# Reading TensorE's moving operands in turn from two halves, in a two-part fp32 transformer on one core

## The chip, the cores and the metric

One Trainium2 chip, of which the program uses one core. The metric is the device time of one execution in microseconds (us). Before the change it is 1760.87 us, the median of three runs (1760.87 to 1761.02).

## What is computed

256 tokens of width 1024 pass through two layers of a first block and two of a second, all in fp32:

```python
def first_block(...):          # twice
    h = rmsnorm(x, g_pre_mix[l])
    z = h @ w_in[l]            # 2660 columns: three attentions' q, k, v, the gates, the low-rank parts
    mix = concatenate([moba, fox, mla, dilated], axis=-1)
    x = x + rmsnorm(mix @ w_out[l], g_post_mix[l])
    h = rmsnorm(x, g_pre_ffn[l])
    f = silu(h @ w_gate[l]) * (h @ w_up[l])          # 2816 columns each
    x = x + rmsnorm(f @ w_down[l], g_post_ffn[l])

def second_block(...):         # twice
    x = x + 0.5 * rms_norm(swiglu(rms_norm(x, ...), ffn1), ...)
    x = x + rms_norm(hybrid_mixer(rms_norm(x, ...), w_in[l], ...), ...)   # gated convolution and pooling
    x = x + 0.5 * rms_norm(swiglu(rms_norm(x, ...), ffn2), ...)
```

Six gated feed-forward networks of width 2816 hold most of the multiplications.

## The kernel before, in words

Every weight matrix is cut, on the host, into units of 128 x 1024 fp32 words (`_layout`), which the kernel reads in the order of their use. A unit goes by DMA into one of five `raw` tiles. ScalarE copies it to fp32r as the high part (`splitter`), and VectorE subtracts that from the raw words to get the low part (`lows`). The high parts lie in tiles `wh` (and `xh` inside a feed-forward network), the low ones in `wl` and `xl`. The activations are split in the same way: `hX` holds the normalized tokens, for each of eight blocks of 128 features 256 words of high part and then 256 of low part; `fH`/`fL`, `tH`/`tL`, `mH`/`mL` and `dH`/`dL` hold later activations.

A product of fp32 accuracy is three fp32r products that accumulate in one PSUM bank. There are three forms of them:

- `mm3` has the tokens as the stationary operand and a stretch of weights (512, 256, 356 or 384 columns) as the moving one: high by high, high by low, low by high. The bank then holds tokens by output columns.
- `pair` has 128 columns of weights as the stationary operand and the tokens as the moving one: 512 columns of `hX` (high and low part) against the high weights, and 256 columns (high part) against the low weights. The bank then holds output columns by tokens, in two halves of 256, which `gather` (and `part` in the feed-forward network) add: ScalarE copies the second half to SBUF, VectorE adds the first half to it.
- `mm3f` does the same as three products of 256 columns, for the pooling groups of the second block.

Each MATMUL has a LDWEIGHTS of its own, which loads its 128 stationary columns.

A feed-forward network takes its 2816 columns in 11 chunks of 256. Chunk 0 is made with `mm3` (`tokens`), chunks 1 to 10 with `pair` (`features`: four banks of eight pairs each), and the products with the down weights (`down`, `mm3`) for chunk c-2 stand behind the features of chunk c. A planner, class `Order`, runs the whole program through a model of the engines when it is built, and writes down each engine's order; it takes the cost of a matmul from its number of columns and of an ACT or DVE instruction from its number of elements. Tiles are taken from lists, the longest idle first.

Where the high part of a unit lies in its `wh` tile depends on what the unit is for. The tile has 16 words (`LEAD`) more than a unit. Units that are stationary operands, counted in `add_units(n, True)`, begin at the tile's start; units that are moving operands begin 16 words, 64 bytes, later. The small tiles `sm` and the tiles `gap` are allocated between the weight tiles so that stationary units of `wh` begin 64 bytes past a multiple of 128 bytes and all others at a multiple:

```python
H = w[0][:, :1024] if i in ahead else w[0][:, LEAD:]
```

Of the kernel before, what the change touches and what calls it, by code (L numbers as in the profile page):

```python
# [11 lines left out]
F32 = mybir.dt.float32  # L12
# [22 lines left out]
ROW_G = 10  # L35
ROW_BG = 12
NSLOT = 9
LEAD = 16
NRAW = 5
NMORE = 5  # L40
TABLE = {AF.Exp: 0, AF.Ln: 1, AF.Silu: 2, AF.Sin: 2, AF.Sigmoid: 3}
# [57 lines left out]
def _meet(a, b):  # L99
# [12 lines left out]
            if not (i0 < j1 and j0 < i1):  # L112
                return False
    return True


class Unit(tuple):
    pass


class Order:
# [160 lines left out]
def body(ctx, tc, x, positions, wu, wm, wq_up, wkv_up, rows, feat, gfeat, cst, cid, out, nsub=99):  # L282
# [41 lines left out]
    def add(o, a, b):  # L324
        return tt(o, a, b, OP.add)
# [52 lines left out]

    hpair = one.tile([P, 16 * S], F32R, name="hX").rearrange("p (k t) -> p k t", k=8)
    hat = [hpair[:, :, :S], hpair[:, :, S:]]  # L380


    smt, wmain = [], []
    for i in range(NSLOT):
        smt += [one.tile([P, 4], F32, name=f"sm{i}_{j}") for j in range(6)]
        wmain.append((one.tile([P, LEAD + 1024], F32R, name=f"wh{i}"), one.tile([P, 1024], F32R, name=f"wl{i}")))
    rawt = [one.tile([P, 1024], F32, name=f"raw{i}") for i in range(NRAW)]
    scrt = [one.tile([P, 512], F32, name=f"scr{i}") for i in range(6)]
    xt = [one.tile([P, D], F32, name=f"x{h}") for h in range(2)]
# [8 lines left out]
    mhalf = one.tile([P, 1], F32, name="mhalf")  # L398
    banks = Slots(ck, [psp.tile([P, 512], F32, name=f"bank{i}") for i in range(8)])
    scr = Slots(ck, scrt)  # L400
    smt += [smp.tile([P, 4], F32, name=f"sm_{i}") for i in range(10)]
    smn = [0]

    def small(n=1):
# [3 lines left out]
    def row_ap(i, n):  # L408
        return bass.AP(tensor=rows.tensor, offset=rows.offset + i * D, ap=[[0, P], [1, n]])

    def mm3(o, lh, ll, wh, wl, start, stop):
        yield mm(o, lh, wh, start, False)
        yield mm(o, lh, wl, False, False)
        yield mm(o, ll, wh, False, stop)

    def mm3f(o, wh, wl, xh, xl, start, stop):
        yield mm(o, wh, xh, start, False)
        yield mm(o, wh, xl, False, False)
        yield mm(o, wl, xh, False, stop)

    def pair(o, wh, wl, x, start, stop):

        yield mm(o, wh, x, start, False)
        yield mm(o[:, :S], wl, x[:, :S], False, stop)

    def gather(bs_, dst=None):
        s = None
        if dst is None:
            s = yield scr
            dst = [s[:, :S], s[:, S:]]  # L430
        for b, d in zip(bs_, dst):
            yield act(d, b[:, S:], AF.Copy)
            yield add(d, d, b[:, :S])
            banks.put(b)
        return s


    more = {"slots": [], "end": 0}
    freed = [Task()]
    plan, ahead = [], set()  # L440
    st = {"dma": 0, "split": 0, "use": 0}
    split_out = {}

# [12 lines left out]
            return B_SPLIT[0] if ahead <= 0 else B_SPLIT[1] if ahead < 2 else B_SPLIT[3] if ck.urgent else B_SPLIT[2]  # L456
        return f

    def lows(i, u):
        H, L = u  # L460
        for _, pp, a, b in plan[i]:
            yield sub(L[:pp, a:b], rawt[i % NRAW][:pp, a:b], H[:pp, a:b], split_bias(i))
        split_out[i] = u
        ck.set(ck.flag("unit", i))
        st["split"] += 1
        issue()
# [14 lines left out]

    def splitter():
        for i in range(len(plan)):
            w = yield from slot(i)
            H = w[0][:, :1024] if i in ahead else w[0][:, LEAD:]
            yield ck.flag("raw", i)
            for _, pp, a, b in plan[i]:
                yield act(H[:pp, a:b], rawt[i % NRAW][:pp, a:b], AF.Copy, split_bias(i))
            if i:
                yield ck.flag("unit", i - 1)  # L490
            u = Unit((H, w[1]))
            u.slot = w
            ck.spawn(lows(i, u))

    def unit():
        i = st["use"]
# [15 lines left out]
    def done(*us):  # L512
        for u in us:
            for w in (u.got if isinstance(u, Units) else [u]):
                (more["slots"] if w.slot[0].name.startswith("xh") else wmain).append(w.slot)
        wake()


# [137 lines left out]
    def ffn(n_, half, nxt, fp):  # L656
# [3 lines left out]
        ck.spawn(gain(n_))  # L660
        ft_ = Slots(ck, [(fp.tile([P, 2, S], F32R, name=f"fH{i}"), fp.tile([P, 2, S], F32R, name=f"fL{i}"))
                         for i in range(3)])
        more["slots"] = [(fp.tile([P, 64 - LEAD], F32, name=f"gap{i}"), fp.tile([P, LEAD + 1024], F32R, name=f"xh{i}"),
                          fp.tile([P, 1024], F32R, name=f"xl{i}"))[1:] for i in range(NMORE)]
        R = fp.tile([P, S], F32, name="R")
        more["end"] = st["use"] + 6 * NCH
        wake()
# [37 lines left out]
        def part(c, i):  # L705

            for m in range(2):
                yield ck.flag("part", n_, c, i, m)
                if m == 0:
                    s = yield scr  # L710
                b = hold.pop((c, i, m))
                d = s[:, m * S:(m + 1) * S]
                yield act(d, b[:, S:], AF.Copy)
                yield add(d, d, b[:, :S])
                banks.put(b)
            hold[c, i] = s

        def fchain(c, g, u):
# [432 lines left out]
    def block2(n_, l, ap, nxt):  # L1151
# [137 lines left out]
        def group(g, tp):  # L1289
            yield tp  # L1290
            b = yield banks
            dH, dL = dT[g]
            H, L = wg.got[g // 2]
            for m in range(2):
                o = b[:, m * S:(m + 1) * S]
                for k in range(2):
                    w = slice((g % 2) * 512 + k * 256 + m * P, (g % 2) * 512 + k * 256 + (m + 1) * P)
                    yield from mm3f(o, H[:, w], L[:, w], dH[:, k, :], dL[:, k, :], k == 0, k == 1)
            ds_.put((dH, dL))
            if g == 3:  # L1300
                done(wg)
            z = yield scr
            for m in range(2):
                j = 2 * g + m
                yield act(z[:, m * S:(m + 1) * S], b[:, m * S:(m + 1) * S], AF.Identity,
                          scale=ft[:, 24 + j:25 + j], bias=bs[:, j:j + 1])
            banks.put(b)
            yield from evac_split(two(z), zX[0][:, 2 * g:2 * g + 2, :], zX[1][:, 2 * g:2 * g + 2, :])
            scr.put(z)
# [80 lines left out]
    subs = subs[:nsub]  # L1390
    nu = 0

    def add_units(n, pairs=False):
        nonlocal nu
        for _ in range(n):
            if pairs:
                ahead.add(len(plan))
            plan.append([(wu[nu // 2][:, (nu % 2) * 1024:(nu % 2 + 1) * 1024], P, 0, 1024)])
            nu += 1

    for kind, l, _ in subs:
        if kind == "f":
            add_units(4)
            for c in range(1, NCH):
                add_units(4, True)
                add_units(2 if c > 1 else 0)
            add_units(4)
        elif kind == "b2":
            add_units(16)
            add_units(34, True)  # L1410
            add_units(24)
        else:
            for i in range(4):
                if l or i:
                    plan.append([(wm[l, i], P, 0, 712)])
                else:
                    plan.append([(wm[l, i][:, a:a + 356], P, a, a + 356) for a in (0, 356)])
            add_units(4 + 4 + 4)
            plan.append([(wq_up[l, :P], P, 0, 384), (wq_up[l, P:], 64, 384, 768)])
            plan.append([(wkv_up[l], P, 0, 512)])  # L1420
            add_units(4 + 2 + 8)
# [55 lines left out]
    return w.reshape(k // P, P, n).transpose(1, 0, 2)  # L1477


def _layout(i):  # L1480
    f = {k: np.ascontiguousarray(v) for k, v in i.items()}
    units = []

    def full(w, n):
        t = _kt(w)
        for c in range(w.shape[1] // n):
            kk = 1024 // n
            for a in range(t.shape[1] // kk):
                units.append(t[:, a * kk:(a + 1) * kk, c * n:(c + 1) * n].reshape(P, 1024))

    def ffn(g, u, d):
        tg, tu, td = _kt(g), _kt(u), _kt(d)

        def gu(c):
            if c:
                for t in (tg, tu):
                    units.extend(t[:, :, c * 256 + j * P:c * 256 + (j + 1) * P].reshape(P, 1024) for j in range(2))
                return
            t = np.concatenate([tg[:, :, c * 256:(c + 1) * 256], tu[:, :, c * 256:(c + 1) * 256]], axis=2)
            units.extend(t[:, 2 * a:2 * a + 2].reshape(P, 1024) for a in range(4))  # L1500

        def dn(c):
            units.extend(td[:, 2 * c + a].reshape(P, 1024) for a in range(2))
        gu(0)
        gu(1)
        for c in range(2, NCH):
# [5 lines left out]
    for l in range(DEPTH):  # L1512
# [6 lines left out]
        t = _kt(f["w_out"][l])  # L1519
        for k in range(0, 8, 2):  # L1520
            for n in range(2):
                units.append(t[:, k:k + 2, n * 512:(n + 1) * 512].reshape(P, 1024))
        ffn(f["w_gate"][l], f["w_up"][l], f["w_down"][l])
    for l in range(DEPTH):
        gu = f["ffn1_w_gate_up_2"][l]
# [2 lines left out]
        full(w[:, 4096:], 512)  # L1528
        for j in range(4):
            for o in (1024, 2048, 0):  # L1530
                full(w[:, o + j * 256:o + (j + 1) * 256], 256)
        t = f["w_pool_group_2"][l].reshape(4, 2, P, 256).transpose(2, 0, 1, 3).reshape(P, 2048)
        units += [t[:, :1024], t[:, 1024:]]
        full(w[:, 3072:4096], 256)
        full(f["w_conv_out_2"][l], 512)
        full(f["w_pool_out_2"][l], 512)
        full(f["w_o_2"][l], 512)
# [2 lines left out]
    wu = np.empty((len(units) // 2, P, 2048), np.float32)  # L1540
    for n, u in enumerate(units):
        wu[n // 2, :, (n % 2) * 1024:(n % 2 + 1) * 1024] = u
    wm = np.stack([_kt(np.ascontiguousarray(f["w_in"][l][:, 1536:1892])).reshape(P, 4, 712).transpose(1, 0, 2)
                   for l in range(DEPTH)])
    rows = np.zeros((ROW_BG + 4, D), np.float32)
    names = [(n, l) for l in range(DEPTH) for n in ("mix", "ffn")]
# [13 lines left out]
    for l in range(DEPTH):  # L1560
        for k in range(3):
# [2 lines left out]
        feat[l, :, 32:40] = f["b_pool_group_2"][l].reshape(8, P).T  # L1564
    cst, cid = _constants()
    return dict(x=f["x"], positions=f["positions"], wu=wu, wm=np.ascontiguousarray(wm),
                wq_up=f["w_mla_q_up"], wkv_up=f["w_mla_kv_up"], rows=rows, feat=feat, gfeat=gfeat, cst=cst, cid=cid)


def _constants():  # L1570
# [35 lines left out]
```

## Time and profile before

| what | value |
|---|---|
| median of three runs | 1760.87 us |
| the profiled execution's own time | 1760.87 us |
| its span, first to last instruction | 1759.1 us |
| granted TensorE clock over the span | 1.000 |
| PE busy | 1749.5 us, 99% |
| DVE busy | 1265.9 us, 72% |
| ACT busy | 1031.8 us, 59% |
| DMA | 187 GB/s in the mean |

PE is the matmuls of TensorE and PEld its weight loads. Busy time is the union of the instructions' spans; matmuls overlap in the profile because each is shown to the end of its pipeline, so the mean duration of a matmul is longer than its place in the stream. How long one matmul holds TensorE is read from the distance between the starts of matmuls that follow each other. In a matmul's names (bank<-hX,wh) the moving operand stands first and the stationary one second.

### The profile page before, as it was taken

The page shows a single profiled execution, that of the slowest core. Times are in us where ns is not written, and L with a number is a line of the kernel's source. Part 1 is how long each engine was busy: PE and PEld are TensorE (multiplying, and loading weights), DVE is VectorE, ACT ScalarE, POOL GpSimd, SP SyncE. Part 2 cuts the span into 40 slices and gives each one's busy share as a digit, 9 for nine tenths or more (in the row PEclk, how much of TensorE's full clock was granted, in tenths as well). Part 3 has the DMA queues.
Part 4 walks back from the last instruction along what each step waited for, and adds up shares of the span by engine and source line. Part 5 has one row for each costly group of instructions (what it writes and reads, how often), then busy time and mean ns, then how long its engine had stood idle before and what let it go on. Part 6 is the DMA issues. An engine that isn't in the chain of part 4 may idle for free.

```text
span 1759.1 us, 25148 instructions
## 1 busy us (share of the span) xinstructions
PE 1749.5 (99%) x9417; PEld 1494.9 (85%) x9417; DVE 1265.9 (72%) x1927; ACT 1031.8 (59%) x1749; POOL 36.9 (2%) x72
## 2 busy tenths in 40 slices
PE   9999999999999999999999999999999999999998
PEld 7788888888888888888888888888888888888887
DVE  6878665877866586656888686668665688868663
ACT  7867553776755475546555575557554655557551
POOL 2000000100000000000000000000000000000000
PEclk9999999999999999999999999999999999999999
DMA  8257664424865376646556486537553655548640
GB/s 285 88 163 245 227 198 136 161 98 129 296 199 192 115 254 209 196 144 204 195 176 193 155 300 198 194 123 261 191 196 131 216 196 175 193 155 302 197 159 24
DMA packets 92283, 328.46 MB, mean 187 GB/s; under 512 B 11008, under 2 KB 12032, under 8 KB 91904
## 3 DMA queue, kind: packets, MB, share of 16 engines
q1 hardware_dynamic: 92160, 326.86, 56.0%
q8 instruction: 73, 1.20, 0.3%
q14 instruction: 50, 0.41, 0.1%
HBM read 325.77 MB, written 1.05 MB: 186 GB/s over the span
## 4 chain that ended last, share of the span: by engine, by line
PE 98%; DMA 1%; ACT 1%; issue 0%; DVE 0%; SPq 0%; DVEq 0%; POOLq 0%; POOL 0%; ACTq 0%
PE bank L297 95%; PE bank L301 3%; DMA raw<-in_wu_dram 0%; ACT wh L314 0%; DMA raw<-in_wm_dram 0%; SPq L372 0%; DVE wl L319 0%; ACT junk L314 0%; ACT hX L314 0%; DVE x L342 0%; DVEq L1602 0%; POOLq L1602 0%; POOL sm L363 0%; DVE ang L342 0%; DVE kf L336 0%
## 5 line engine op out<-in xcount | busy, mean ns | idle before, releaser
L319 DVE TENSOR_TENSOR wl<-raw,wh 128x1024 fp32r<-128x1024 f32 (+1 forms) x472 | 565.5, 1207 | 163.4 <-ACT wh L314 157.6
L297 PE MATMUL bank<-hX,wh 128*128 128x512 f32 x1736 | 594.9, 390 | 0.0
L314 ACT ACTIVATE wh<-raw 128x1024 fp32r<-128x1024 f32 (+1 forms) x472 | 489.0, 1043 | 119.0 <-DMA raw<-in_wu_dram 53.9
L297 PE MATMUL bank<-hX,wl 128*128 128x256 f32 x1736 | 479.9, 276 | 0.0
L297 PEld LDWEIGHTS bank<-hX,wh 128*128 128x128 f32 x1736 | 325.9, 188 | 67.4
L297 PEld LDWEIGHTS bank<-hX,wl 128*128 128x128 f32 x1736 | 325.9, 188 | 1.5
L297 PE MATMUL bank<-wh,hX 128*128 128x512 f32 (+2 forms) x960 | 299.1, 386 | 0.1
L314 ACT ACTIVATE scr<-bank 128x256 f32<-128x256 f32 x288 | 109.3, 380 | 280.7 <-PE bank L297 280.7
L297 PE MATMUL bank<-hX,xh 128*128 128x512 f32 x696 | 239.0, 389 | 0.0
L297 PEld LDWEIGHTS bank<-wh,hX 128*128 128x128 f32 x960 | 177.4, 189 | 32.4 <-issue 1.5
L319 DVE TENSOR_TENSOR scr<-scr,bank 128x256 f32<-128x256 f32 x288 | 120.8, 419 | 112.0 <-ACT scr L314 111.4
L319 DVE TENSOR_TENSOR xl<-raw,xh 128x1024 fp32r<-128x1024 f32 x139 | 168.8, 1223 | 39.9 <-ACT xh L314 38.3
L297 PE MATMUL bank<-hX,xl 128*128 128x256 f32 x696 | 192.2, 276 | 0.0
L297 PE MATMUL bank<-wl,hX 128*128 128x512 f32 (+2 forms) x480 | 184.7, 385 | 0.5 <-DVE wl L319 0.5
L314 ACT ACTIVATE xh<-raw 128x1024 fp32r<-128x1024 f32 x139 | 145.1, 1055 | 20.6 <-DMA raw<-in_wu_dram 13.6
L297 PEld LDWEIGHTS bank<-hX,xh 128*128 128x128 f32 x696 | 130.6, 188 | 27.3
L297 PEld LDWEIGHTS bank<-hX,xl 128*128 128x128 f32 x696 | 130.7, 188 | 0.6
L297 PE MATMUL bank<-wl,fH 128*128 128x512 f32 x320 | 125.1, 391 | 0.0
L297 PE MATMUL bank<-wh,fH 128*128 128x512 f32 x320 | 125.1, 391 | 0.0
L297 PE MATMUL bank<-wh,fL 128*128 128x512 f32 x320 | 124.5, 389 | 0.0
L297 PEld LDWEIGHTS bank<-wl,hX 128*128 128x128 f32 x480 | 90.7, 189 | 16.1 <-DVE wl L319 0.8
L297 PE MATMUL bank<-xl,fH 128*128 128x512 f32 x208 | 81.5, 392 | 0.0
(148 smaller groups left out, 1940.3 us busy)
## 6 DMA issues: line engine op xcount, KB each, us to landing
raw<-in_wu_dram SPq DMA_DIRECT2D x596, 512.0 KB, 4.7
gpost<-in_rows_dram SPq DMA_DIRECT2D x10, 512.0 KB, 7.0
raw<-in_wm_dram SPq DMA_DIRECT2D x7, 356.0 KB, 4.0
bg<-in_rows_dram SPq DMA_DIRECT2D x2, 1024.0 KB, 4.5
x<-in_x_dram SPq DMA_DIRECT2D x4, 256.0 KB, 4.9
out_dram<-x SPq DMA_DIRECT2D x4, 256.0 KB, 2.0
raw<-in_wkv_up_dram SPq DMA_DIRECT2D x2, 256.0 KB, 3.4
raw<-in_wq_up_dram SPq DMA_DIRECT2D x2, 192.0 KB, 4.8
```

Of the source, the lines that this page charges most:

```text
L297: return Op("e", c, (o,), (l, r), lambda: nc.tensor.matmul(o, l, r, start=start, stop=stop), bias, half)
L301: return Op("e", 0.1094, (o,), (i,), lambda: nc.tensor.transpose(o, i, idt[:, :P]))
L314: return Op("a", c, outs, ins, lambda: nc.scalar.activation(o, i, f, **kw), bias_, None, f)
L319: lambda: nc.vector.tensor_tensor(o, a, b, op=op), bias)
```

## The change

Every fp32r matmul now reads its moving operand in turn from the first and the second half of its columns (first column of the one, first column of the other, second of the one, and so on). In `mm3` the halves are of the weights: 256 words (1024 bytes) apart for 512 columns, 128 words (512 bytes) for 256. In `pair` the high and the low 256 tokens are each read in turn from halves 128 words apart. The number of columns, the stationary operands and the output (contiguous columns of the bank) stay.

So that the banks of `mm3` come out in their usual order, the host lays out weights that are moving operands with the even columns first and the odd ones behind them (`_turns`); units that are stationary operands stay as they were. The banks of `pair` and `mm3f` come out with tokens 0, 128, 1, 129 and so on; the ACT and DVE instructions that read them (`added`, and the pooling groups' activation) read every second element (`inorder`) and write two halves (`halved`).

The placing of the high parts goes: no `LEAD`, no `ahead`, `sm` in a pool of their own. The tiles `wh` and `wl` now all begin at multiples of 128 bytes, `xh` and `xl` 64 bytes past one. The order of the instructions on each engine and queue stays as it was, instruction by instruction: the planner's costs know neither steps nor addresses.

```diff
-LEAD = 16
...
-    smt, wmain = [], []
-    for i in range(NSLOT):
-        smt += [one.tile([P, 4], F32, name=f"sm{i}_{j}") for j in range(6)]
-        wmain.append((one.tile([P, LEAD + 1024], F32R, name=f"wh{i}"), one.tile([P, 1024], F32R, name=f"wl{i}")))
+    wmain = [(one.tile([P, 1024], F32R, name=f"wh{i}"), one.tile([P, 1024], F32R, name=f"wl{i}"))
+             for i in range(NSLOT)]
...
+    def turns(v):
+        return view(v).rearrange("p (a t) -> p t a", a=2)
+
+    def inorder(b):
+        return b.rearrange("p (t a) -> p a t", a=2)
+
+    def halved(d):
+        return d.rearrange("p (a t) -> p a t", a=2)
+
     def mm3(o, lh, ll, wh, wl, start, stop):
+        wh, wl = turns(wh), turns(wl)
         yield mm(o, lh, wh, start, False)
         yield mm(o, lh, wl, False, False)
         yield mm(o, ll, wh, False, stop)
 
     def mm3f(o, wh, wl, xh, xl, start, stop):
+        xh, xl = turns(xh), turns(xl)
...
     def pair(o, wh, wl, x, start, stop):
 
-        yield mm(o, wh, x, start, False)
-        yield mm(o[:, :S], wl, x[:, :S], False, stop)
+        yield mm(o, wh, x.rearrange("p (c a t) -> p c t a", c=2, a=2), start, False)
+        yield mm(o[:, :S], wl, turns(x[:, :S]), False, stop)
+
+    def added(b, d):
+        yield act(halved(d), inorder(b[:, S:]), AF.Copy)
+        yield add(halved(d), halved(d), inorder(b[:, :S]))
+        banks.put(b)
...
-            H = w[0][:, :1024] if i in ahead else w[0][:, LEAD:]
...
-        more["slots"] = [(fp.tile([P, 64 - LEAD], F32, name=f"gap{i}"), fp.tile([P, LEAD + 1024], F32R, name=f"xh{i}"),
-                          fp.tile([P, 1024], F32R, name=f"xl{i}"))[1:] for i in range(NMORE)]
+        more["slots"] = [(fp.tile([P, 1024], F32R, name=f"xh{i}"), fp.tile([P, 1024], F32R, name=f"xl{i}"))
+                         for i in range(NMORE)]
...
-                yield act(z[:, m * S:(m + 1) * S], b[:, m * S:(m + 1) * S], AF.Identity,
+                yield act(halved(z[:, m * S:(m + 1) * S]), inorder(b[:, m * S:(m + 1) * S]), AF.Identity,
...
+def _turns(w):
+
+    return np.ascontiguousarray(np.concatenate([w[..., 0::2], w[..., 1::2]], axis=-1))
...
-            units.extend(t[:, 2 * a:2 * a + 2].reshape(P, 1024) for a in range(4))
+            units.extend(_turns(t[:, 2 * a:2 * a + 2]).reshape(P, 1024) for a in range(4))
```

## Rows read from the trace of the kernel before

**Rows 1.** The profile's head and its busy times.
```profile
span 1759.1 us, 25148 instructions
...
PE 1749.5 (99%) x9417; PEld 1494.9 (85%) x9417; DVE 1265.9 (72%) x1927; ACT 1031.8 (59%) x1749; POOL 36.9 (2%) x72
```

**Rows 2.** Chain that ended last: shares by engine, and its longest piece (start, length).
```profile
PE 98%; DMA 1%; ACT 1%; issue 0%; DVE 0%; SPq 0%; DVEq 0%; POOLq 0%; POOL 0%; ACTq 0%
...
143.81 164.37 PE bank L297 x881
```

**Rows 3.** Waits of PE, all of them: total us, times, longest.
```profile
PE bank L301 <- DMA x<-in_x_dram: 1.3, 1, 1.3
PE bank L297 <- DVE mhalf L1435: 1.2, 1, 1.2
PE bank L297 <- DVE wl L319: 0.5, 1, 0.5
PE bank L297 <- DVE lf L342: 0.4, 1, 0.4
```

**Rows 4.** Groups of PE by form: count, busy us, mean ns, idle before.
```profile
L297 PE MATMUL bank<-hX,wh 128*128 128x512 f32 x1736 | 594.9, 390 | 0.0
L297 PE MATMUL bank<-hX,wl 128*128 128x256 f32 x1736 | 479.9, 276 | 0.0
...
L297 PE MATMUL bank<-hX,xl 128*128 128x256 f32 x696 | 192.2, 276 | 0.0
...
L297 PE MATMUL bank<-wl,mH 128*128 128x512 f32 x68 | 27.0, 397 | 0.0
```

**Rows 5.** Timeline in a feed-forward network, 512 moving columns: two starts, 18 matmuls apart.
```profile
299.85 0.39 PE L297 MATMUL bank<-xh,fH 128*128 128x512 f32 x1
...
303.93 0.39 PE L297 MATMUL bank<-xh,fH 128*128 128x512 f32 x1
```

**Rows 6.** Timeline in a feed-forward network, pairs: two starts, ten pairs apart.
```profile
700.52 0.39 PE L297 MATMUL bank<-hX,wh 128*128 128x512 f32 x1
...
703.92 0.39 PE L297 MATMUL bank<-hX,wh 128*128 128x512 f32 x1
```

**Rows 7.** Timeline in the second first-block layer, 256 moving columns alone: starts, 21 apart.
```profile
393.44 0.28 PE L297 MATMUL bank<-wl,hX 128*128 128x256 f32 x1
...
395.96 0.28 PE L297 MATMUL bank<-wl,hX 128*128 128x256 f32 x1
```

**Rows 8.** fp32 passes of 256 columns: eight in a row (timeline), and their group.
```profile
365.80 1.89 PE L297 MATMUL bank<-qk,qk 65*128 65x256 f32 x8
...
L297 PE MATMUL bank<-qk,qk 65*128 65x256 f32 x16 | 4.0, 385 | 0.0
```

**Rows 9.** Groups of DVE and ACT by form: the readers of the pairs' banks, and 512 elements.
```profile
L319 DVE TENSOR_TENSOR scr<-scr,bank 128x256 f32<-128x256 f32 x288 | 120.8, 419 | 112.0 <-ACT scr L314 111.4
L319 DVE TENSOR_TENSOR scr<-scr,R 128x512 f32<-128x512 f32 x76 | 52.2, 687 | 0.5
...
L314 ACT ACTIVATE scr<-bank 128x256 f32<-128x256 f32 x288 | 109.3, 380 | 280.7 <-PE bank L297 280.7
L314 ACT ACTIVATE fH<-scr 128x512 fp32r<-128x512 f32 x60 | 37.8, 630 | 66.3 <-DVE scr L319 66.3
```

**Rows 10.** Busy us by stretch: PE, PEld, DVE, ACT, POOL, then granted clock, DMA share, GB/s.
```profile
300.00:600.00 300.00, 300.00 (x1667) 253.81 (x1666) 215.88 (x385) 189.96 (x365) 9.24 (x18) 1.00 0.53 175
```

More of the change, by code (lines that the diff above doesn't have):

```diff
@@ L114, in _meet @@
     return True
-class Unit(tuple):
-    pass
 class Order:
@@ L400, in body @@
     scr = Slots(ck, scrt)
-    smt += [smp.tile([P, 4], F32, name=f"sm_{i}") for i in range(10)]
+    smt = [smp.tile([P, 4], F32, name=f"sm{i}") for i in range(72)]
     smn = [0]
@@ L431, in gather @@
         for b, d in zip(bs_, dst):
-            yield act(d, b[:, S:], AF.Copy)
-            yield add(d, d, b[:, :S])
-            banks.put(b)
+            yield from added(b, d)
         return s
@@ L439, in body @@
     freed = [Task()]
-    plan, ahead = [], set()
+    plan = []
     st = {"dma": 0, "split": 0, "use": 0}
@@ L457, in split_bias, with lows @@
         return f
-    def lows(i, u):
-        H, L = u
+    def lows(i, H, L):
         for _, pp, a, b in plan[i]:
             yield sub(L[:pp, a:b], rawt[i % NRAW][:pp, a:b], H[:pp, a:b], split_bias(i))
-        split_out[i] = u
+        split_out[i] = (H, L)
         ck.set(ck.flag("unit", i))
@@ L483, in splitter @@
         for i in range(len(plan)):
-            w = yield from slot(i)
-            H = w[0][:, :1024] if i in ahead else w[0][:, LEAD:]
+            H, L = yield from slot(i)
             yield ck.flag("raw", i)
@@ L490, in splitter @@
                 yield ck.flag("unit", i - 1)
-            u = Unit((H, w[1]))
-            u.slot = w
-            ck.spawn(lows(i, u))
+            ck.spawn(lows(i, H, L))
     def unit():
@@ L514, in done @@
             for w in (u.got if isinstance(u, Units) else [u]):
-                (more["slots"] if w.slot[0].name.startswith("xh") else wmain).append(w.slot)
+                (more["slots"] if w[0].name.startswith("xh") else wmain).append(w)
         wake()
@@ L711, in part @@
                 b = hold.pop((c, i, m))
[L712 to L715, printed above, removed]
+                yield from added(b, s[:, m * S:(m + 1) * S])
             hold[c, i] = s
@@ L1391, in body, with add_units @@
     nu = 0
-    def add_units(n, pairs=False):
+    def add_units(n):
         nonlocal nu
         for _ in range(n):
-            if pairs:
-                ahead.add(len(plan))
             plan.append([(wu[nu // 2][:, (nu % 2) * 1024:(nu % 2 + 1) * 1024], P, 0, 1024)])
@@ L1402, in body @@
         if kind == "f":
[L1403 to L1407, printed above, removed]
+            add_units(66)
         elif kind == "b2":
-            add_units(16)
-            add_units(34, True)
-            add_units(24)
+            add_units(74)
         else:
@@ L1482, in _layout, with full @@
     units = []
-    def full(w, n):
+    def full(w, n, turns=True):
         t = _kt(w)
@@ L1488, in full @@
             for a in range(t.shape[1] // kk):
-                units.append(t[:, a * kk:(a + 1) * kk, c * n:(c + 1) * n].reshape(P, 1024))
+                u = t[:, a * kk:(a + 1) * kk, c * n:(c + 1) * n]
+                units.append((_turns(u) if turns else u).reshape(P, 1024))
     def ffn(g, u, d):
@@ L1499, in gu @@
             t = np.concatenate([tg[:, :, c * 256:(c + 1) * 256], tu[:, :, c * 256:(c + 1) * 256]], axis=2)
-            units.extend(t[:, 2 * a:2 * a + 2].reshape(P, 1024) for a in range(4))
+            units.extend(_turns(t[:, 2 * a:2 * a + 2]).reshape(P, 1024) for a in range(4))
         def dn(c):
-            units.extend(td[:, 2 * c + a].reshape(P, 1024) for a in range(2))
+            units.extend(_turns(td[:, 2 * c + a].reshape(P, 2, 512)).reshape(P, 1024) for a in range(2))
         gu(0)
@@ L1521, in _layout @@
             for n in range(2):
-                units.append(t[:, k:k + 2, n * 512:(n + 1) * 512].reshape(P, 1024))
+                units.append(_turns(t[:, k:k + 2, n * 512:(n + 1) * 512]).reshape(P, 1024))
         ffn(f["w_gate"][l], f["w_up"][l], f["w_down"][l])
@@ L1530, in _layout @@
             for o in (1024, 2048, 0):
-                full(w[:, o + j * 256:o + (j + 1) * 256], 256)
+                full(w[:, o + j * 256:o + (j + 1) * 256], 256, False)
         t = f["w_pool_group_2"][l].reshape(4, 2, P, 256).transpose(2, 0, 1, 3).reshape(P, 2048)
         units += [t[:, :1024], t[:, 1024:]]
-        full(w[:, 3072:4096], 256)
+        full(w[:, 3072:4096], 256, False)
         full(f["w_conv_out_2"][l], 512)
@@ L1542, in _layout @@
         wu[n // 2, :, (n % 2) * 1024:(n % 2 + 1) * 1024] = u
-    wm = np.stack([_kt(np.ascontiguousarray(f["w_in"][l][:, 1536:1892])).reshape(P, 4, 712).transpose(1, 0, 2)
+    wm = np.stack([_kt(_turns(f["w_in"][l][:, 1536:1892])).reshape(P, 4, 712).transpose(1, 0, 2)
                    for l in range(DEPTH)])
@@ L1566, in _layout @@
     return dict(x=f["x"], positions=f["positions"], wu=wu, wm=np.ascontiguousarray(wm),
-                wq_up=f["w_mla_q_up"], wkv_up=f["w_mla_kv_up"], rows=rows, feat=feat, gfeat=gfeat, cst=cst, cid=cid)
+                wq_up=_turns(f["w_mla_q_up"]), wkv_up=_turns(f["w_mla_kv_up"]), rows=rows, feat=feat, gfeat=gfeat, cst=cst, cid=cid)
 def _constants():
```

## The prediction

> **What bounds the kernel now.** I begin with the head of the profile [rows 1]: PE is busy for 1749.5 of 1759.1 us, and has 9417 matmuls and as many weight loads. A busy PE may still wait inside, so the chain that ended last comes next [rows 2]: 98% of it is PE, and one of its pieces is 881 matmuls in 164 us without a stop, an interval of 186 ns per matmul of 512 or 256 columns. The waits of PE add up to 3.4 us in all [rows 3]. So the time is the sum of the intervals at which TensorE takes one matmul after the other. Nothing else sets the end, and the order of the instructions doesn't change. The question is only what one matmul holds the engine for, before and after.
>
> The mean durations in the groups don't tell that, since matmuls overlap there; their counts do [rows 4]. There are sixteen fp32r groups of 512 columns, from 1736 to 68 matmuls, 5852 together. The pairs' second matmuls, of 256 columns, are 1736 and 696, so 2432. Another 192 of 256 columns stand outside pairs, and 120 of 356 or 384.
>
> The intervals come from the timeline, by starts:
>
> - 512 columns: 18 steps in 4.08 us, 226.7 ns [rows 5]. At 2.4 GHz, the level of the granted clock 1.00 [rows 10], 512 columns are 213.3 ns, so 13.4 ns are extra.
> - Pairs: 10 steps in 3.40 us, 340.0 ns [rows 6]. Less 226.7 this leaves 113.3 ns for 256 columns, where 106.7 would be the columns: 6.6 extra.
> - 256 columns outside pairs: 21 steps in 2.52 us, 120.0 ns [rows 7]. Here the extra is 13.3, as with 512 columns.
> - A plain fp32 pass takes two cycles for a column: eight in 1.89 us, of which the last shows 385 ns, so (1890 - 385)/7 = 215.0 ns for 256 columns, or 512 cycles [rows 8]. Its extra is 1.7 ns.
>
> I read the following out of this. The extra time is nothing fixed to a matmul, since the slower fp32 passes have 1.7 ns of it. It doesn't grow with the columns either (256 outside pairs cost as much extra as 512). It is about 32 cycles for each matmul, so for each weight load of 128 words, when the moving operand streams one word per cycle. And it halves in the pairs, half of whose weights lie 64 bytes beside the others. So it looks like the weight load and the moving stream meeting at one place in SBUF, which depends on addresses and so perhaps on the order of reading. That is my reading of the intervals; no row names the cause.
>
> [...]
>
> **The change, part by part.**
>
> *Moving operands in turn.* No row shows a moving operand with steps, so its price is bounded. From below: each matmul falls to the extra of the fp32 pass. 512 columns go from 226.7 to 215.0, 11.7 x 5852 = 68.5 us. Pairs' 256 columns go from 113.3 to 106.7 + 1.7 = 108.4, 4.9 x 2432 = 11.9 us. The others of 256 go from 120.0 to 108.4, 11.6 x 192 = 2.2 us; the 120 of 356 or 384 I leave out. Together that is 82.6 us. If the last 1.7 ns went too, 8476 x 1.7 = 14.4 us more. From above: a column costs what it does in the fp32 pass, two cycles, which is the nearest row for a stream that can't be read at full rate. Then 512 columns take 430.0, 203.3 x 5852 = 1189.7 us more; pairs' 256 take 215.0, 101.7 x 2432 = 247.3 more; the others 95.0 x 192 = 18.2 more: 1455 us in all. I take the lower side, because the intervals say that the stall depends on where two streams stand to each other. A contiguous stream stays for 16 columns inside 64 bytes, the distance that made the difference between 120.0 and 113.3; a stream in turn leaves its place at each column. That argues for a shorter meeting, not for none, so I count nine tenths of 82.6: 74 us.
>
> *Weights of pairs back at multiples of 128 bytes.* This undoes the placing to which I put the 113.3 ns. If order makes the meetings short, it costs nothing; if it doesn't, 120.0 - 113.3 = 6.7 ns x 2432 = 16.3 us come back, or 11.6 if the 696 with weights in `xh`, which still begin 64 bytes past a multiple, keep theirs.
>
> *Banks read at every second element.* 288 reads each by ACT (380 ns) and DVE (419 ns) [rows 9], and 16 activations for the pooling groups. No row has such steps. At best they cost nothing. At worst each element counts twice: on DVE 512 elements take 687, so 256 more are 268 ns and 288 x 0.268 = 77 us; on ACT 630 - 380 = 250 ns, 72 us. Both lie beside PE's work: in a stretch of 300 us DVE is busy for 215.9 and ACT for 190.0 [rows 10], and at most a sixth of the calls fall in each of the six feed-forward networks, so 13 us more on DVE in a stretch of 164 us [rows 2], of which it idles 46 at that share. The products that use the result come a whole chunk later in the order. I count 0. If that cover went, PE would wait for `fH`, and at most the 77 us would show.
>
> *Supply of weights.* A faster PE asks for units sooner. DVE's 216 of 300 us would become 216 of 287, so it, ACT and the DMA (share 0.53) still have room [rows 10]. I count 0.
>
> *Layout on the host, small tiles.* Same bytes and same DMAs: 0.
>
> The sum is made against the profiled execution, whose own time, 1760.9, is the median. 1760.9 - 74 = **1687 us**.
>
> **The rivals.**
>
> *The stream can't change place at every column.* The mechanism: a read serves several neighbouring words of a contiguous stream; in turn, it serves one, and TensorE takes a column every second cycle, as in the fp32 passes. The place is every fp32r matmul, and the point from which it decides is any interval above 226.7 ns. Time: 1760.9 + 1455 = **3216 us**. For it: the fp32 passes show that the engine does run at that rate. Against it: they do so with contiguous reads, so theirs is a cost of arithmetic, and no row ties it to reading. Chance 0.19.
>
> [...]
>
> *The stall is the weight load's alone.* The order of the moving reads does nothing, and what counts is where the weights lie. Then only the loss of the placing remains, in the pairs: 1760.9 + 11.6 to 16.3, **1775 us**. It decides if 512 columns stay at 227 ns. For it: the halving from 120.0 to 113.3 goes with the weights' place. Against it: 512 columns keep 13.4 ns though in pairs their weights begin at the same 64 bytes, so place alone doesn't explain it. Chance 0.15.
>
> *Half the stall goes.* The two halves stand at the same distance to multiples of 128 bytes, so they can still meet the weights, half as often: 1760.9 - 41 = **1720 us**. Chance 0.12.
>
> *Nothing happens.* The new stream gains in one place what the pairs lose in the other, or no read meets another: **1761 us**. Chance 0.06.
>
> **How the numbers follow.** The forecast of 1687 gets 0.48; it is the only case for which all four intervals speak. A measurement of this kernel tells 0.2%, 3.5 us, from no change. Faster are the forecast and the half, 0.60; same is 0.06; slower are the two rivals, 0.34. The range goes from 1760.9 - 82.6 - 14.4 = 1664, rounded to 1662, to 1780, just above the loss of the placing. It leaves out the rival at 3216 with its 0.19. The forecast's own range, as cases of both signs hold much, is 1664 to 1705.
>
> **What would show it.** In the changed kernel's timeline, 18 matmuls of 512 columns in 3.87 to 3.9 us instead of 4.08, and ten pairs in 3.23 to 3.28 instead of 3.40; PE's waits still a few us, and DVE's reads of the banks below 690 ns. The forecast is wrong if 18 steps still take 4.08 us (then look at the pairs, for 3.47), or if they take more (then 7.7 is the second cycle). PE waiting for `fH` or `wl` by more than 10 us would mean that the hidden work isn't hidden.

## The result, and the profile after

The changed kernel takes 1688.61 us (median of four runs, 1688.39 to 1689.79) against 1760.94 for the kernel before: a ratio of 0.959, 95% interval 0.9574 to 0.9607. It is 72.3 us faster; 1687 was forecast.

The head and the busy times of the profile after, against [rows 1]:

```profile
span 1688.0 us, 25148 instructions
...
PE 1676.5 (99%) x9417; PEld 1494.6 (89%) x9417; DVE 1258.6 (75%) x1927; ACT 1027.2 (61%) x1749; POOL 35.8 (2%) x72
```

The same instructions, and PE still busy for 99% of the span. PE gave up 73.0 us of busy time; DVE and ACT work nearly as long as before (7.3 and 4.6 us less). The longest piece of the chain that ended last (start, length, count), against [rows 2, 3]:

```profile
139.96 157.34 PE bank L292 x881
```

And the longest waits of PE (total us, count, longest), against the same rows:

```profile
PE bank L296 <- DMA x<-in_x_dram: 2.3, 1, 2.3
PE bank L292 <- DVE mhalf L1428: 1.2, 1, 1.2
PE bank L292 <- DVE lf L337: 1.0, 1, 1.0
PE bank L296 <- DVE w L331: 0.8, 1, 0.8
PE bank L292 <- DVE wl L314: 0.3, 1, 0.3
```

The same 881 matmuls take 157.34 us instead of 164.37, and the waits went from 3.4 to 5.6 us. So the gain is in the intervals inside a stream without stops, and no new wait took its place. The timeline shows them: in the feed-forward network 18 steps of 512 columns, then ten pairs; and 24 steps of 256 columns outside pairs. They answer to [rows 5 to 7]:

```profile
284.19 0.38 PE L292 MATMUL bank<-xh,fH 128*128 128x512 f32 x1
...
288.07 0.38 PE L292 MATMUL bank<-xh,fH 128*128 128x512 f32 x1
...
674.77 0.38 PE L292 MATMUL bank<-hX,wh 128*128 128x512 f32 x1
...
678.05 0.38 PE L292 MATMUL bank<-hX,wh 128*128 128x512 f32 x1
...
380.23 0.28 PE L292 MATMUL bank<-wl,hX 128*128 128x256 f32 x1
...
382.91 0.28 PE L292 MATMUL bank<-wl,hX 128*128 128x256 f32 x1
```

18 steps in 3.88 us instead of 4.08, ten pairs in 3.28 instead of 3.40, and 256 columns outside pairs in 2.68/24 = 111.7 ns instead of 120.0. Per step that is 215.6 ns for 512 columns. Averaged over all pairs in the trace, a pair takes 218.4 + 109.1 = 327.5 ns.

The readers of the pairs' banks, with every second element, against [rows 9]:

```profile
L314 DVE TENSOR_TENSOR scr<-scr,bank 128x256 f32<-128x256 f32 x288 | 120.4, 418 | 97.2 <-ACT scr L309 97.1
...
L309 ACT ACTIVATE scr<-bank 128x256 f32<-128x256 f32 x288 | 109.2, 379 | 245.4 <-PE bank L292 245.3
```

418 ns for 419 and 379 for 380: reading a bank in steps of two elements costs these engines nothing here.

### The profile page after: what moved, and what is told of

It reads as the page before. It is cut to its first block, busy times and chain, and to the rows that moved or that the text cites. A ratio compares the mean times of both kernels' runs of the same rounds, so it can differ in the third digit from the quotient of the medians.

```text
span 1688.0 us, 25148 instructions
## 1 busy us (share of the span) xinstructions
PE 1676.5 (99%) x9417; PEld 1494.6 (89%) x9417; DVE 1258.6 (75%) x1927; ACT 1027.2 (61%) x1749; POOL 35.8 (2%) x72
## 4 chain that ended last, share of the span: by engine, by line
PE 96%; ACT 1%; DMA 1%; DVE 1%; issue 1%; SPq 0%; DVEq 0%; POOLq 0%; POOL 0%; ACTq 0%
PE bank L292 93%; PE bank L296 3%; DMA raw<-in_wu_dram 1%; ACT wh L309 1%; DMA raw<-in_wm_dram 0%; DVE wl L314 0%; ACT hX L309 0%; ACT L309 0%; SPq L367 0%; ACT junk L309 0%; DVE sm L342 0%; ACT qk L309 0%; DVE x L337 0%; DVE w L314 0%; DVEq L1601 0%
## 5 line engine op out<-in xcount | busy, mean ns | idle before, releaser
L292 PE MATMUL bank<-hX,wh 128*128 128x512 f32 x1736 | 572.7, 382 | 0.0
L292 PE MATMUL bank<-hX,wl 128*128 128x256 f32 x1736 | 473.7, 273 | 0.0
L292 PEld LDWEIGHTS bank<-hX,wl 128*128 128x128 f32 x1736 | 333.2, 192 | 1.0
L292 PE MATMUL bank<-wh,hX 128*128 128x512 f32 (+2 forms) x960 | 287.2, 375 | 0.0
L309 ACT ACTIVATE scr<-bank 128x256 f32<-128x256 f32 x288 | 109.2, 379 | 245.4 <-PE bank L292 245.3
L292 PE MATMUL bank<-hX,xh 128*128 128x512 f32 x696 | 230.3, 382 | 0.0
L292 PE MATMUL bank<-wl,hX 128*128 128x512 f32 (+2 forms) x480 | 179.5, 374 | 0.3 <-DVE wl L314 0.3
L292 PE MATMUL bank<-wh,fH 128*128 128x512 f32 x320 | 121.6, 380 | 0.0
L292 PE MATMUL bank<-wl,fH 128*128 128x512 f32 x320 | 121.4, 380 | 0.0
L292 PE MATMUL bank<-xh,fH 128*128 128x512 f32 x208 | 79.1, 380 | 0.0
```

The source lines that it names most:

```text
L292: return Op("e", c, (o,), (l, r), lambda: nc.tensor.matmul(o, l, r, start=start, stop=stop), bias, half)
L309: return Op("a", c, outs, ins, lambda: nc.scalar.activation(o, i, f, **kw), bias_, None, f)
```

## The experiments

Three theories go through the expectations. Theory A is the prediction's: the weight load and the moving stream meet at one place in SBUF. Theory B: a contiguous moving stream loses time by itself, in proportion to its columns. Theory C: only the weights' place counts.

### Order and placing apart, in the whole kernel

Three variants of the changed kernel. The first reads everything in order, so that only the placing is gone:

```diff
     def turns(v):
-        return view(v).rearrange("p (a t) -> p t a", a=2)
+        return view(v)
...
-    return np.ascontiguousarray(np.concatenate([w[..., 0::2], w[..., 1::2]], axis=-1))
+    return np.ascontiguousarray(w)
```

(and `inorder`, `halved` and `pair` likewise). Expected:

> All reads in order as in the kernel before, with the placing of the changed one: the step that only takes the 64 bytes away. Theory A with the placing as I read it: 512 columns stay at 227, the pairs' 256 columns go from 113.3 to 120, so 1761 + 12 to 16 = 1773 to 1777 us. Theory B: 256 columns stay at 113 and the time at 1761 us. If the placing was worth more than the pairs' halving, above 1780.

Measured: 1787.38 us, ratio 1.0147 (1.0132 to 1.0163), so the placing alone is worth 26.4 us, above what the prediction had for it. Ten pairs take 3.49 us, 349 ns each:

```profile
149.93 0.39 PE L292 MATMUL bank<-hX,xh 128*128 128x512 f32 x1
...
153.42 0.39 PE L292 MATMUL bank<-hX,xh 128*128 128x512 f32 x1
```

Over the trace, the pairs' 512 columns went from 227 to 232 ns and their 256 from 113.3 to 117.4: both parts of a pair had gained from the placing, not the 256 alone. Matmul by matmul against the trace of the kernel before, the pairs account for 22.2 us and the 512 columns outside pairs for 3.9. That second loss goes with a move that the change made besides: the tokens' tiles `fH`, `tH` and `mH`, stationary operands of `mm3`, began at multiples of 128 bytes and now begin 64 bytes past one, and matmuls such as bank<-wh,fH went from 228 to 230 ns.

The second variant leaves only the pairs in order:

```diff
-        yield mm(o, wh, x.rearrange("p (c a t) -> p c t a", c=2, a=2), start, False)
-        yield mm(o[:, :S], wl, turns(x[:, :S]), False, stop)
+        yield mm(o, wh, x, start, False)
+        yield mm(o[:, :S], wl, x[:, :S], False, stop)
```

(and `added` reads and writes in order again). Expected:

> The changed kernel with the pairs' tokens read in order again (mm3 and mm3f still in turn). Their 2432 pairs should cost 340 ns (with the placing's gain) or 347 (without) instead of 327.4, so 1688.6 + 31 = 1719 us if order alone counts (theory B), or 1688.6 + 47 = 1736 us under theory A with the placing gone.

Measured: 1748.82 us, ratio 0.9926 (0.9911 to 0.9941), slower than either figure, since the placing's loss in the pairs was set too low: a pair takes 234.4 + 117.6 = 352.0 ns here, not 347. With the first variant the gain divides: reading the weights of `mm3` and `mm3f` in turn gives 1787.4 - 1748.8 = 38.6 us, reading the pairs' tokens in turn 1748.8 - 1688.6 = 60.2 us. Together 98.8, of which 26.4 replace what the placing had given, and 72.3 are new. The division is good to some 6 us only: the same pairs, read in order, take 349.5 ns in the first variant and 352.0 here, and 2432 x 2.5 ns are 6.1 us. Why they differ isn't shown.

The third puts the placing of the kernel before back under the turned reads (`LEAD`, `ahead`, and the tiles between, as in the lines that the change took out):

> The changed kernel with the 64 bytes of the kernel before back in place, so turned reads and placing together. If turned reads leave no meeting (theory A), the placing is worth nothing: 1688.6 us, pairs at 327 ns. If the 2.5 ns that 512 columns in pairs still cost above those in mm3 (218.3 for 215.8) come from the weights' place (theory C), they go: 2432 x 2.5 = 6 us less, 1682.5 us.

Measured: 1690.89 us (1688.87 to 1691.86), ratio 0.9597 (0.9581 to 0.9613), with pairs at 218.4 + 109.1 ns as without it; that is 2.3 us more than without the placing, where theory C wanted 6 less. Read in turn, the weights' place no longer matters, and the 2.5 ns that 512 columns in pairs cost above the others don't come from it.

### Moving orders, one by one

A program without the network runs 40 matmuls of each kind in a row, with four stationary slices by turns. Its series differ in the moving operand's pattern or in the weights' place, for instance

```python
("turn", lambda t: turn(t, 512, 1), weights(0)),     # "p (a t) -> p t a", a=2
("two", lambda t: turn(t, 512, 2), weights(0)),      # turns every 2 columns
("evens", lambda t: step(t, 512, 2), weights(0)),    # "p (t a) -> p a t", a=2
```

> Leaves out the whole network: 29 series of 40 fp32r matmuls (and one of bf16) that differ in one thing each, named by their moving tile; read are the intervals between starts. Theory A (the weight load and the moving stream meet at one place in SBUF, so the extra belongs to the weight load and ends with a moving order that doesn't stay at a place): contig (512 columns in order) 227 ns; half and quart (64 and 32 stationary words for 128) 221 and 218, since fewer words are loaded; turn 216; two, four, eight, sixteen, thirty (turns every 2, 4, 8, 16, 32 columns) rise from 217 to 227; evens (step of 8 bytes) in between, stepd and stepp (steps of 16 and 64 bytes) 216. Theory B (a contiguous stream alone loses one cycle in 16 columns, whatever weights are loaded): half and quart stay at 227, short (256 columns) 113 instead of A's 120, wherever the weights lie. Theory C (the weights' place alone): contigb, contigc, contigd (weights 64, 16, 32 bytes further) differ from contig by up to 11 ns, and turn differs from turnb. Weights read with steps of 8, 16 and 32 bytes (wtwo, wfour, weight) change the interval under A and C, not under B. [...]

In the timeline each series is one row (start, length, count). A length holds the slow first step and the last matmul's pipeline; the intervals in the text are means of the steps from the fourth on. The single bf16 matmul between two series is left out of the rows.

```profile
7.42 9.38 PE L40 MATMUL bank<-contig,ws 128*128 128x512 f32 x40 [1.42 <-ACT contig L36]
...
45.05 9.40 PE L40 MATMUL bank<-half,ws 128*64 128x512 f32 x40
54.33 9.45 PE L40 MATMUL bank<-quart,ws 128*32 128x512 f32 x40
...
73.24 8.88 PE L40 MATMUL bank<-turn,ws 128*128 128x512 f32 x40
82.00 8.88 PE L40 MATMUL bank<-turnb,ws 128*128 128x512 f32 x40
90.76 13.57 PE L40 MATMUL bank<-two,ws 128*128 128x512 f32 x40
104.21 10.24 PE L40 MATMUL bank<-four,ws 128*128 128x512 f32 x40
...
143.52 18.41 PE L40 MATMUL bank<-evens,ws 128*128 128x512 f32 x40
161.81 18.68 PE L40 MATMUL bank<-stepd,ws 128*128 128x512 f32 x40
180.37 17.56 PE L40 MATMUL bank<-stepp,ws 128*128 128x512 f32 x40
...
240.93 8.80 PE L40 MATMUL bank<-bfmove,wb 128*128 128x512 bf16 x39
```

In turn costs 215.8 ns, exactly what bf16 in order costs. But theory A's figures fail in three places. Turning every 2, 4, 8, 16 or 32 columns gives 333, 250, 243, 240 and 237 ns, all worse than in order (227); so a stream that leaves its place more often isn't better for that. And steps of 8, 16 and 64 bytes cost 453, 461 and 433 ns, the double, where A wanted a gain. Half or a quarter of the stationary words leave 230 and 232 ns: the extra isn't a cost per word loaded. Theory B, which wanted 227 there, fails with them, and with 256 columns, which take 119.9 ns or, with the weights 64 bytes further, 113.3. Theory C holds in part: in order, weights 16, 32 or 64 bytes further cost 233 ns for 227 with 512 columns, and gain with 256; in turn there is no difference (turn, turnb). Weights read in steps of 8, 16 and 32 bytes make the ordered stream slower too, 236, 235 and 244 ns.

The last seven series are pairs as in the kernel. In turn they take 327.5 ns at each of four placings of the two weights. In order they take 351.2 with both at multiples of 128 bytes, 346.7 with the high part 64 bytes past one, as in the kernel before, and 353.2 with both past one. So the placing's gain shows here as well, but at half its size: the 340 ns of the kernel before were not met.

### Every second column a stream of its own

What turning at each column has that no other pattern has: columns 0, 2, 4 and so on walk through one half word by word, and columns 1, 3, 5 through the other. In order, each of the two walks in steps of two words. That is theory D, and the next program was made for it; theory E is that the distance between neighbours counts. Its patterns are written as steps and counts:

```python
("turneight", F32R, full, ((2, 256), (512, 2))),
("turnsixt", F32R, full, ((1, 2), (4, 128), (512, 2))),
("nearsixt", F32R, full, ((8, 64), (1, 4), (4, 2))),
("one", F32R, weights(ws, 0, 1), ((1, 512),)),
```

> Leaves out the whole network: 21 series of 40 matmuls of 512 columns, named by their moving tile. Theory D: columns 0, 2, 4... and columns 1, 3, 5... are two streams, and what counts is the step inside one of them: 4 bytes is free (216 ns), 8 bytes costs a little (227 to 234), 16 bytes and more costs the double (430 to 460). Theory E: what counts is the distance between neighbours in the whole stream: 4 bytes nearly free, 8 to 64 bytes double, far halves free. Series and D / E: turneight (halves in turn, each with steps of 8 bytes) 230 / 216; turnsixt (steps of 16 bytes) 430 or more / 216; quarters (four quarters in turn, so each stream changes place every time) 333 or more / 216; nearthirty, nearsixt, neareight (turns between words 32, 16 and 8 bytes apart) 216, 216, 230 / 430 or more; twice (each word read twice) 216 / no statement; gap and backturn (halves 1088 and 2048 bytes apart) 216 / 216; bf16: bfcontig 216, bffour (steps of 4 bytes, 8 in a stream) 227, bfeight (8, 16 in a stream) and bfsixt (16, 32) 430, bfturneight (halves in turn, 8 in a stream) 227 / E has bffour near 216 and bfturneight at 216. Theory A, that the weight load causes the extra of an ordered stream: one and eights (1 and 8 stationary words) 216; D and E: 227 or more, as contig.

Rows of this program, as above:

```profile
7.21 9.36 PE L40 MATMUL bank<-contig,ws 128*128 128x512 f32 x40
16.45 9.46 PE L40 MATMUL bank<-one,ws 128*1 128x512 f32 x40
...
61.32 8.88 PE L40 MATMUL bank<-twice,ws 128*128 128x512 f32 x40
70.08 9.34 PE L40 MATMUL bank<-turneight,ws 128*128 128x512 f32 x40
79.30 18.28 PE L40 MATMUL bank<-turnsixt,ws 128*128 128x512 f32 x40
97.46 11.56 PE L40 MATMUL bank<-quarters,ws 128*128 128x512 f32 x40
...
117.66 8.88 PE L40 MATMUL bank<-nearsixt,ws 128*128 128x512 f32 x40
126.42 9.34 PE L40 MATMUL bank<-neareight,ws 128*128 128x512 f32 x40
135.64 18.28 PE L40 MATMUL bank<-evens,ws 128*128 128x512 f32 x40
```

Theory D meets its fp32r figures but one. Steps of 4 bytes inside a stream: 215.8 ns, with the two streams 2048, 1088, 1024, 32 or 16 bytes apart, or on the same words (twice). Steps of 8 bytes: 227.2 (turneight, neareight), as in order. Steps of 16 bytes: 451.1 (turnsixt), as in evens. Theory E falls with turnsixt and nearsixt. The miss is quarters: a stream that changes its place at each word takes 283 ns, less than the 333 expected. Theory A falls with one: a single stationary word leaves the extra of an ordered stream, 231.7 ns (eight words: 231.1). Of the bf16 series the first three go with theory D: in order (4 bytes inside a stream) 215.8 ns, bffour (8 bytes) 225.8 and bfeight (16 bytes) 453.3. The other two, bfsixt at 900 and bfturneight at 653, don't, and are taken up below.

The whole kernel can tell D from E too. Its pairs read in turn between words 16 bytes apart, in blocks of eight (and `added` reads the banks back in the same blocks):

```diff
-        yield mm(o, wh, x.rearrange("p (c a t) -> p c t a", c=2, a=2), start, False)
-        yield mm(o[:, :S], wl, turns(x[:, :S]), False, stop)
+        yield mm(o, wh, x.rearrange("p (b a t) -> p b t a", a=2, t=4), start, False)
+        yield mm(o[:, :S], wl, x[:, :S].rearrange("p (b a t) -> p b t a", a=2, t=4), False, stop)
```

> The changed kernel, with the pairs' tokens read in turn between words 16 bytes apart, inside blocks of eight, instead of between halves 512 bytes apart (mm3 and mm3f unchanged; the banks are read back in blocks). Theory D (what counts is the step inside the stream of every second column): 327.5 ns per pair as now, so 1688.6 us within 0.3%. Theory E (the halves' distance keeps the reads apart): pairs at the double, 2432 x 320 ns more, 2467 us. If ACT and DVE lose by reads with one dimension more, their 288 copies and adds show it, 380 and 419 ns before.

Measured: 1689.2 us (1688.93 to 1689.86), ratio 0.9591 (0.9575 to 0.9607), pairs at 218.4 + 109.1 ns, and 418 and 378 ns for the banks' readers. The halves are one way to write the order; whether they lie 512 or 16 bytes apart does nothing.

### What is left in the pairs, and bf16

> Leaves out the whole network: series of 32 matmuls named by their moving tile, with 24 ordered bf16 matmuls (keep) between them so that the clock stays up. bfsixt (bf16, steps of 32 bytes within a stream) 450 at the full clock. bf16 in turn: theory D as it stands puts bfturn (2 bytes in a stream) and bfnear at 216, bfturnfour (4 bytes) at 216, bfturneight (8 bytes) at 227; theory F, that two neighbouring bf16 words are fetched as one, puts all four well above 216 (bfturneight was 653 at the lower clock, some 327 at the full one). eighths and nearquart (eight and four places in turn, so each stream changes place at every word) 283 or more, as quarters. For the 2.5 ns left in pairs: if the next weights' load is longer than 256 columns, short (256 columns in turn, 128 stationary words) 111.7 and shorthalf (64 words) 109, and pairs with 64 stationary words (both) 215.8 + 109.1 = 324.9 instead of 327.5; if it is fixed to a matmul of 256 columns, no difference.

```profile
7.27 15.66 PE L40 MATMUL bank<-bfturn,wb 128*128 128x512 bf16 x32 [0.36 <-ACT bfturn L36]
...
27.95 7.07 PE L40 MATMUL bank<-bfnear,wb 128*128 128x512 bf16 x32
...
40.04 17.44 PE L40 MATMUL bank<-bfturnfour,wb 128*128 128x512 bf16 x32
...
125.67 3.92 PE L40 MATMUL bank<-short,ws 128*128 128x256 f32 x32
...
134.43 3.85 PE L40 MATMUL bank<-shorthalf,ws 128*64 128x256 f32 x32
```

256 columns in turn take 111.7 ns with 128 stationary words and 109.2 with 64, and the pairs with 64 words 216.0 + 109.0. So the 2.5 ns left in each pair go with the 128 stationary words. That the load of the next ones is a little longer than 256 moving columns fits these figures; it isn't shown beyond them, since 64 stationary words also make 64 rows of output for 128, and in a pair the 2.5 ns stand in the interval of the 512 columns.

For bf16 theory D is wrong as it stands. Turning between far halves costs 484 ns (bfturn), 540 (bfturnfour) and 653 (bfturneight), against 216 in order; only turns 8 bytes apart (bfnear) keep 216. Theory F, that neighbouring bf16 words are fetched together, said so of the far ones, but it wanted bfnear well above 216 as well, and bfturneight at some 327. bfsixt takes 900 ns, not 450. What rule bf16 follows stays open. eighths take 487 ns and nearquart 268.5, where 283 was the least expected.

### How the extra of an ordered stream goes with its columns

> Leaves out the whole network: series of 40 fp32r matmuls of 320, 384, 448 and 512 columns, in order with the weights at a multiple of 128 bytes and 64 bytes past it (far), and in turn. The earlier intervals of 256 and 512 columns in order (113.3 or 120 ns, 227 or 233.3) are 17/16 of the columns at 2.4 GHz, with 0 or 16 cycles on top. Theory B with a place term: 320, 384, 448, 512 columns take 141.7, 170.0, 198.3, 226.7 ns, or 6.7 more each at one of the two places; so the gap to the turned series (135.8, 162.5, 189.2, 215.8) grows with the columns, from about 6 to 11 ns at the better place. Theory A as the prediction had it (32 cycles for each weight load): 146.7, 173.3, 200.0, 226.7, a constant gap of some 11 ns. If the place that counts is that of moving and stationary operand to each other, bothfar (both 64 bytes further) equals fourfull and movefar equals fourfullfar. If the place term belonged to the loading of many words, onefar (one word) would have none.

```profile
7.40 6.13 PE L40 MATMUL bank<-three,ws 128*128 128x320 f32 x40
...
19.40 5.68 PE L40 MATMUL bank<-threeturn,ws 128*128 128x320 f32 x40
24.96 7.19 PE L40 MATMUL bank<-threehalf,ws 128*128 128x384 f32 x40
32.03 7.32 PE L40 MATMUL bank<-threehalffar,ws 128*128 128x384 f32 x40
39.23 6.75 PE L40 MATMUL bank<-threehalfturn,ws 128*128 128x384 f32 x40
45.86 8.50 PE L40 MATMUL bank<-fourless,ws 128*128 128x448 f32 x40
54.23 8.33 PE L40 MATMUL bank<-fourlessfar,ws 128*128 128x448 f32 x40
62.45 7.81 PE L40 MATMUL bank<-fourlessturn,ws 128*128 128x448 f32 x40
...
97.59 9.42 PE L40 MATMUL bank<-movefar,ws 128*128 128x512 f32 x40
106.89 9.33 PE L40 MATMUL bank<-bothfar,ws 128*128 128x512 f32 x40
116.09 9.54 PE L40 MATMUL bank<-movefarther,ws 128*128 128x512 f32 x40
```

320, 384 and 448 columns take 146.5, 173.3 and 206.5 ns (far: 146.7, 176.7, 202.2) and in turn 135.8, 162.5 and 189.2. The gap is 11, 11 and 17 ns, with 512 columns 12 or 17: between 11 and 17 for 320 to 512 columns. Theory B falls. The constant of theory A stands roughly (448 columns take 6.5 ns more than it had), but not its link to the words loaded: one word (onefar) takes 231 ns, at this place as at the other (one).

Which place counts isn't settled. Both operands 64 bytes further is 226.7 again (bothfar), so it is in part the one operand's to the other. But the moving one alone 64 bytes further takes 229.0 here (movefar) and 233.3 in the program on every second column (its last series, offset), and 128 bytes further, at a multiple of 128 again, it takes 232.4 (movefarther) and not 226.7.

## Why the prediction was right, point by point

**What bounds the kernel.** Right: intervals of a stream without stops set the time, 881 matmuls fell by 7.03 us in all, and the matmuls that the change doesn't touch took 3 us longer.

**Moving operands in turn, 74 us.** The size was right. The two traces hold the same 9417 matmuls in the same order, so their intervals can be compared one by one. 512 columns outside pairs gave 39.3 us and in pairs 21.7: 61.0 where the full term was 68.5. Pairs' 256 columns gave 9.9 for 11.9, the others of 256 1.4 for 2.2, and those of 356 and 384, which were left out, 1.8. That is 74 us; all other matmuls took 3 us longer, 2.2 of it in longer waits, which leaves the 71.1 us between the two spans. What the tenth stood for turned out to be mostly two things. The floor is 215.8, not the 215.0 taken from the plain fp32 passes, 0.8 x 5852 = 4.7 us, and each pair keeps 2.5 ns, 6.1 us, with its 128 stationary words. The prediction took the tenth for "a shorter meeting, not for none", so that it came out at 74 is luck. The 2.4 GHz behind the 213.3 ns stands in no row, [rows 10] have 1.00; the turned series bear it out, with 192 columns more in 80.0 ns more (135.8 to 215.8), 0.417 ns for a column.

The reason behind the choice was wrong in its main part. "The weight load and the moving stream meeting at one place" explains neither that one stationary word leaves the extra nor that turns every two columns are slower. What the runs show is that fp32r reads behave as if every second column were a stream of its own, which with 512 columns costs 215.8 ns in steps of 4 bytes, the same as bf16 in order, pays 11 to 17 ns more per matmul (320 to 512 columns) in steps of 8 and the double, 451 ns, in steps of 16. That describes the runs and isn't a cause, and streams that change their place at each word lie outside it: 333 ns (two), 283 (quarters), 268.5 (nearquart), 487 (eighths). The step "a contiguous stream stays for 16 columns inside 64 bytes" fails: two streams 16 bytes apart, or on the same words, are as fast as far ones. That the low side came true, and not the double, rests on the step inside each stream, which the prediction didn't weigh; its direction was right for another reason than it gave. That the extra is per matmul and hardly grows with the columns was right. What the 11 to 17 ns of an ordered stream are stays open; a stream without any load beside it wasn't tried.

**Placing.** "If order makes the meetings short, it costs nothing" held: 1690.9 with it, 1688.6 without. The price named for the other case, 11.6 to 16.3 us, was too low; it is 26.4, because the placing had helped both matmuls of a pair (22.2 us), and `mm3` as well (3.9).

**Banks, supply, layout.** Counted 0, and nearly 0: 418 and 379 ns, and 2.2 us more of PE's waits.

**The rivals.** The one that doubles each column is true of other orders: evens, stepd and stepp take 433 to 461 ns. Its mechanism, a read that serves several neighbouring words, was a supposition; no run shows it. What saved this order goes, as the series show it, with the step inside each stream of every second column: 215.8 ns with 4 bytes there, 451.1 with 16. The rival of the weights' place alone is out by 215.8 for 512 columns, though under ordered reads the place does count: contigb against contig, where it alone differs, is 233.3 against 226.7 ns in a settled stream. Half the stall (1720 us) and no change are out by the time itself.

## What to carry to other kernels

In an fp32r kernel that is bound by TensorE, compare the distance of matmul starts with the columns, 0.417 ns each at the granted clock of 1.00 here; the dozen ns more that such a matmul took here, in order, were had back by an order in which every second column walks word by word through another place, and a place 16 bytes away did as well. It is no general rule for strided reads: steps of 8, 16 and 64 bytes in the plain order doubled the time (453, 461 and 433 ns for 227), turns every 2 to 32 columns lost (333 to 237 ns), and bf16 between far halves went from 216 to 484 ns. Where the output comes out permuted, permute the weights on the host or let ACT and DVE read the banks in steps; neither cost device time here (418 and 379 ns for the banks' readers, 419 and 380 before).

## What the runs showed of the hardware beyond that

The granted clock fell from 1.00 to 0.50 in the stretches of the slow bf16 series, though the profile shows PE busy throughout: a mean of 0.61 and 0.57 over bfturneight and bfsixt, and 1.00 again later.

```profile
62.50:83.70 21.20, 21.05 (x33) 3.72 (x33) 0.00 (x0) 0.00 (x0) 0.00 (x0) 0.61 0.00 0
90.70:119.80 29.10, 28.98 (x33) 4.14 (x33) 0.00 (x0) 0.00 (x0) 0.00 (x0) 0.57 0.00 0
134.40:138.30 3.90, 3.88 (x34) 3.67 (x34) 0.00 (x0) 0.00 (x0) 0.00 (x0) 1.00 0.00 0
```

(Columns as in [rows 10].) By the page's 40 slices the clock is 0.9 or more up to 67.9 us, within the first of them, and between 0.5 and 0.6 in the 19 us from there on. The intervals of these series are 653 and 900 ns here, and the same in the program on every second column, whose page has the lower clock in all of bfturneight and all but the start of bfsixt; so there the granted clock didn't set the pace. That the reading of the moving operand did is the author's inference: its pattern is all that differs from the ordered bf16 series at 215.8 ns.

Once an ordered stream has settled, the intervals of most series come to a multiple of 6.67 ns in the mean, 16 times the 0.417 ns of a column in turn: 113.3, 120.0, 146.7, 173.3, 206.7, 226.7 and 233.3 (not so 176.7 and 202.2). In turn they don't: 135.8, 162.5, 189.2 and 215.8 are the columns at 0.417 ns and 2.5 ns more.
